# Two room buffers for factors and weights, two steps read ahead, and a late norm vector

## The chip, the cores and the metric

The kernel runs on one core of a Trainium2 chip. The metric is the device time of one launch in microseconds (us), the median over several executions. The engines of the core are called PE (matrix engine, with its weight loads listed apart), VectorE (DVE), ScalarE (ACT), GpSimd (POOL) and SyncE (SP), whose queue issues most of the transfers.

## What is computed

One decoder layer over 1024 prompt tokens and 64 sample tokens, model width 1024. Of the reference these lines matter here:

```
o_diff = diff_attention(...); o_nsa = nsa_attention(...)
mix = jnp.concatenate([o_diff, o_nsa], axis=-1) @ w_out
x = x + rms_norm(mix, g_post_mix)
hm = rms_norm(x, g_pre_mlp)
ff = jnp.square(jax.nn.relu(hm @ w_up)) @ w_down
x = x + rms_norm(ff, g_post_mlp)
```

w_out is 1024 x 1024, w_up 1024 x 4096, w_down 4096 x 1024. All of it is float32.

## The kernel before

Every float32 product is done with operands split in a high and a low part (high by a copy on ScalarE, low by a subtraction on VectorE), and as three matmuls (high-high, high-low, low-high).

The attention fills the time up to about 990 us. Its outputs are written to the DRAM tensor mixT by small stores from tiles named ot. Then three stages follow, and their instructions are interleaved by the framework: it tracks which tile a buffer holds, makes the next user of a buffer wait for the last one of it, and puts each engine's instructions in an order of its own, so that work of the next stage stands among the last of the one before.

1. The out projection, function `phase_out`. There are nine token tiles t = 0..8 (t = 8 has the 64 sample tokens). `weight(k)` loads 128 rows of w_out to a raw tile ur (4 buffers) and splits it in two halves n = 0, 1 of 512 columns: eight k times two n are held as "us" (n = 0, k < 5) or "w" tiles. `front(t)` loads the tile's columns of mixT into a "us" tile of the room pool `rr` and splits it to xm. `prod(t, n)` makes 24 matmuls into the PSUM tile C, and for n = 0 also loads the residual input x into a room tile "us". `post(t)` squares C on ScalarE, normalises, adds x, stores the sum to the DRAM tensor x1d, normalises again to ctmp, and has PE transpose it (T) into xf, the input of the next product.
2. The up product, `phase_up`: a seven-product scheme of fast matrix multiplication over quarters. The x side has factors xc[i, p] for two halves of the tokens p = 0 and 1, seven i each, made by `x_factor` from xf. The w side has a factor W[j, i] per column block j, made from raw w_up tiles and kept in a ring of "us" tiles. Its matmuls write tiles Va to Vd (first block) and Ua to Ud, and its results (squared ReLU) are stored as hF.
3. The down product, `phase_down`, of the same scheme: 96 whole steps of 24 matmuls (Dn) and 32 half ones. A step needs wf (from w_down, tiles eq, qe and q) and hf (from hr, a strip of hF read back; eh is one read early). `load_w` loads blocks of w_down; a dictionary `gate` says at which step each later block may start, by a copy that waits for that step. `load_h(n)` loads hr for step n, and `factor(n)` makes wf and hf.

The x_factor calls for i = 3 and 2 of p = 0 (the last two in the order UORD) stand at the start of phase_up's tail, behind the last post:

```
for i in UORD[5:]:
    self.x_factor(i, 0)
    factor(0, i)
close(0)
```

and their tiles lie in the pool xcb, which opens after `phase_out` has closed its pools.

Of the kernel before, what the change touches and what calls it, by code (L numbers as in the profile page):

```python
# [17 lines left out]
F32 = mybir.dt.float32  # L18
# [45 lines left out]
def f32(ap):  # L64
    return ap.bitcast(F32)
# [60 lines left out]
class Kern:  # L126
# [1108 lines left out]
    def phase_out(self, cl):  # L1235
# [1 line left out]

        nc, A = self.nc, self.A
        w_out = A["w_out"][0]
        ws = []  # L1240
        xins, mhs, pss = {}, {}, {}
        rr = self.rr

        def weight(k):
            raw = rr.tile([P, 4, 256], F32, name="ur", bufs=4).rearrange("p a n -> p (a n)")
            nc.sync.dma_start(raw, w_out[k * P:(k + 1) * P])
            ws.append([])
            for n in range(2):
                c = slice(n * 512, n * 512 + 512)
                if n == 0 and k < 5:  # L1250
                    w = self.wa.tile([P, 2, 4, P], FR, name="us", bufs=5).rearrange("p a k n -> p a (k n)")
                else:
                    w = self.wp.tile([P, 2, 512], FR, name="w")
                self.act_copy(w[:, 0], raw[:, c])
                nc.vector.tensor_sub(w[:, 1], raw[:, c], f32(w[:, 0]))
                ws[-1].append(w)

        def front(t):
            m = self.tok(t)[2]
            mx = rr.tile([P, 2, 4, P], F32, name="us", bufs=3).rearrange("p a b n -> p (a b) n")  # L1260
            nc.sync.dma_start(mx[:, :, :m], self.mixT[:, t * P:t * P + m].rearrange("(k p) t -> p k t", p=P))
            mh = rr.tile([P, 2, 4, QT], FR, name="xm", bufs=2).rearrange("p a b n -> p (a b n)")[:, :2 * KC * P]
            mh = mhs[t] = mh.rearrange("p (a k n) -> p a k n", a=2, k=KC)
            self.act_copy(mh[:, 0, :, :m], mx[:, :, :m])
            nc.vector.tensor_sub(mh[:, 1, :, :m], mx[:, :, :m], f32(mh[:, 0, :, :m]))
            pss[t] = []
# [15 lines left out]
        def prod(t, n):  # L1282
            m = self.tok(t)[2]
            ps = self.psC.tile([P, 512], F32, name="C", tag="C")
            pss[t].append(ps)
            if n == 0:
                xins[t] = rr.tile([P, 2, 4, P], F32, name="us", bufs=3).rearrange("p a b n -> p (a b n)")
                nc.sync.dma_start(xins[t][:m], self.xsrc(t))
            cnt = 0
            for k in range(KC):  # L1290
                for a, b in ((0, 0), (0, 1), (1, 0)):
                    nc.tensor.matmul(ps[:m], mhs[t][:, a, k, :m], ws[k][n][:, b],
                                     start=cnt == 0, stop=cnt == 3 * KC - 1)
                    cnt += 1
# [48 lines left out]
            prod(t, 0)  # L1343
        for t in range(NT - 1, NT + 1):
            prod(t, 1)
            post(t)
            if t < NT:
                self.up_open()
                for i in UORD[:5]:
                    self.up_factor(0, i)  # L1350
# [44 lines left out]
    def up_open(self):  # L1395

        nc, A, rp = self.nc, self.A, self.rr
        w_up = A["w_up"][0]
        raws, S2 = {}, {}
        W = self.W = {}  # L1400

        def load(j):
            raws[j] = []
            for kh in range(2):
                r = rp.tile([P, 4, 256], F32, name="ur", bufs=4)
                nc.sync.dma_start(r, w_up[kh * 512:kh * 512 + 512, j * 256:j * 256 + 256]
                                  .rearrange("(k p) c -> p k c", p=P))
                raws[j].append(r)

        def factor(j, i):  # L1410
            if j == NJ:
                return
            r0, r1 = raws[j]
            q = (r0[:, :, 0:P], r1[:, :, 0:P], r0[:, :, P:256], r1[:, :, P:256])
            n = len(W) % 8
            W[j, i] = w = (self.wa if n < 5 else rp).tile([P, 2, 4, P], FR, name="us", bufs=5 if n < 5 else 3)
            if i == 5:
                S2[j] = rp.tile([P, 4, P], F32, name="s2", bufs=1)
            self.left(q, i, w, nc.vector, nc.vector, S2.get(j, 0))

        self.up_load, self.up_factor = load, factor
        load(0)
        load(1)

    def phase_up(self, close):
# [85 lines left out]
            nxt(2)  # L1511

        for i in UORD[5:]:
            self.x_factor(i, 0)
            factor(0, i)
        close(0)

# [10 lines left out]
    def down_open(self):  # L1528

        nc = self.nc  # L1530
        self.eq = self.early.tile([P, 1, 512], F32, name="eq")
        nc.sync.dma_start(self.eq, self.A["w_down"][0].rearrange("(s e p) c -> e p s c", e=2, p=P)[0, :, 0:1, 0:512])
        self.eh = []
        for sb in range(1):
            h = self.early.tile([P, HT], F32, name=f"eh{sb}")
            nc.sync.dma_start(h, self.hF[DORD[0], sb * P:sb * P + P])
            self.eh.append(h)

    def phase_down(self, qe, qp, fp, psD):
# [19 lines left out]
        def load_w(q, c, gate=None):  # L1559

            r, e = q % 2, q // 2
            s0, s1 = (max(c * 4 - 3, 0), min(c * 4 + 1, NB)) if q == 0 else (c * 4, c * 4 + 4)
            if q == 0 and c == 0:
                t = self.eq
            elif q == 0 and c < 3:
# [8 lines left out]
                (nc.scalar if q == 0 and c < 3 else nc.sync).dma_start(t, w_dn[e, :, s0:s1, r * 512:r * 512 + 512])  # L1574


        def factor(n):
            if n >= len(hr):
                return
            i, sb, p = hr[n]  # L1580
            load_h(n + 4)
            a11, a21, a12, a22 = (quarter.get((q, sb)) for q in range(4))
            v = nc.vector
            if i == 6:
# [39 lines left out]

            return qp.tile([P, 4, 512], F32, name="q03") if n % 3 == 2 else qe.tile([P, 4, 512], F32, name="qe", bufs=2)

        gate = {0: (0, 2), 3: (0, 3), 7: (0, 4)}
        for k, (q, c) in enumerate([(q, c) for q in (1, 3, 2) for c in range(4)]):
            gate[9 + (k % 4) * 4 + (k // 4) * NB] = (q, c)
        R.update(enumerate(self.eh))  # L1630
        load_w(0, 0)
        load_h(1, nc.scalar)
        load_w(0, 1)
        load_h(2, nc.scalar)
        load_h(3, nc.scalar)
        factor(0)
        factor(1)
        for k in range(4):
            acc[k] = qp.tile([P, 4, HT], F32, name=f"acc{k}")
        gp = qp.tile([P, D], F32, name="gpm")  # L1640
# [10 lines left out]
        for n, (i, sb, p) in enumerate(hr):  # L1651
            if n in gate:
                load_w(*gate[n], gate=f32(F[n][0][:, 1, 0:1]))
            if n == 5 * NB:
                nc.sync.dma_start(gp, A["g_post_mlp"].to_broadcast([P, D]))
            factor(n + 2)
            w, h = F.pop(n)
# [228 lines left out]
    def go(self):  # L1886
        with self.pool("base") as base:
# [50 lines left out]
            with ExitStack() as es:  # L1938
# [2 lines left out]

                self.rr = e(self.pool("rr", side="right"))
                self.wa = e(self.pool("wa", side="right"))
                xca = e(self.pool("xca", side="right"))
                self.xstack = [e(ExitStack()) for _ in range(2)]
                self.xc = {}
# [3 lines left out]

                up0 = e(ExitStack())
                self.psU0 = up0.enter_context(self.pool("psU0", side="right", psum=True))
                with self.pool("w2", 11) as self.wp, self.pool("cl") as cl, \
                        self.pool("psC", 3, psum=True) as self.psC, self.pool("psT2", 1, psum=True) as self.psT:
                    self.xtile = xtile
                    self.xca = xca
# [1 line left out]
                early = ExitStack()  # L1958
                self.early = early.enter_context(self.pool("early"))
                with self.pool("xcb") as xcb, ExitStack() as ps:  # L1960
                    for i, p in [(i, 1) for i in UORD[:2]] + [(i, 0) for i in UORD[5:]] + [(i, 1) for i in UORD[2:5]]:
                        xtile(xcb, i, p)
                    for i in UORD[5:]:
                        xtile(self.rr, i, 1, "xm", 2)

# [77 lines left out]
```

## Time and profile before

| | |
|---|---|
| runs before, us | 1824.03 median of 3 (1822.09 to 1831.58) |
| profiled execution, us | 1819.73 |
| its span, us | 1817.9 |
| mean granted clock of PE | 0.969 of full speed |
| PE busy, us (share of the span) | 1709.6 (94%) |
| VectorE busy | 1137.8 (63%) |
| ScalarE busy | 865.4 (48%) |

The profiled execution's time is that of the launch; the span runs from its first to its last instruction. The projection takes from about 972 to 1086 us, the up product from 1075 to 1444, the down product from there to 1803. Of the rows below, a timeline row gives the start in us, the busy time, the engine, the line, the instruction, its tiles (what is written <- what is read) and a count where several run on end; in brackets stands how long the engine was idle ahead of it and who released it.

### The profile page before, as it was taken

The numbers are of one execution on the slowest core, as the hardware profiler recorded it, in microseconds if no ns is written. First come the engines' busy times: TensorE is split into PE (matmuls) and PEld (weight loads), VectorE is DVE, ScalarE is ACT, GpSimd is POOL, SyncE is SP. The second block draws the span as 40 slices with busy tenths as digits, with TensorE's granted clock in tenths as the row PEclk, the third lists the DMA queues.
The fourth block names the chain that finished last, engine by engine and source line by source line (L and its number), as shares of the span: only waits on it lengthen the run. The fifth ranks groups of instructions, "written<-read, shape, count | busy, mean of one in ns | idle before, by whom it ended". The sixth has DMA issues, their size and how long they took to land. (4 is left out here: it accounts for less than half of the span.)

```text
span 1817.9 us, 33390 instructions
## 1 busy us (share of the span) xinstructions
PE 1709.6 (94%) x12155; PEld 1487.3 (82%) x12155; DVE 1137.8 (63%) x2716; ACT 865.4 (48%) x2188; POOL 273.3 (15%) x517
## 2 busy tenths in 40 slices
PE   7689999999998999999989997999999899999997
PEld 7678776677666778787877877999999899999996
DVE  5357667767863575667665478566666456847665
ACT  5244446456762364555555355444444334543442
POOL 1133335334330121212110000000000000000000
PEclk9888899999998999999998998999999999999999
DMA  7531000000203243424245322434443465554334
GB/s 195 115 75 45 14 14 24 7 4 23 58 7 113 86 145 88 120 81 130 65 134 182 129 91 80 140 133 151 145 145 110 159 214 168 177 165 115 106 118 150
DMA packets 193919, 191.92 MB, mean 106 GB/s; under 512 B 32562, under 2 KB 152986, under 8 KB 193754
## 3 DMA queue, kind: packets, MB, share of 16 engines
q1 hardware_dynamic: 191114, 185.10, 33.2%
q10 hardware_dynamic: 2640, 4.68, 0.8%
q8 instruction: 96, 1.57, 0.4%
q14 instruction: 69, 0.57, 0.1%
HBM read 133.75 MB, written 55.97 MB: 104 GB/s over the span
## 5 line engine op out<-in xcount | busy, mean ns | idle before, releaser
L337 PE MATMUL M<-w,xt 128*128 128x384 f32 (+4 forms) x1584 | 293.4, 330 | 15.4 <-ACT natk L139 12.6
L1665 PE MATMUL Dn<-hf,wf 128*128 128x272 f32 x2304 | 292.4, 290 | 10.1 <-ACT hf L139 8.1
L1665 PEld LDWEIGHTS Dn<-hf,wf 128*128 128x128 f32 x2304 | 291.0, 190 | 11.4 <-ACT hf L139 8.4
L337 PEld LDWEIGHTS M<-w,xt 128*128 128x128 f32 (+1 forms) x1584 | 243.8, 191 | 30.2 <-ACT natk L139 13.5
L427 ACT ACTIVATE p<-S,nm 128x512 f32<-128x512 f32 (+3 forms) x288 | 159.9, 561 | 87.8 <-DVE nm L422 48.8
L418 DVE TENSOR_REDUCE nm<-S 128x1 f32<-128x512 f32 (+3 forms) x288 | 148.1, 527 | 59.1 <-PE S L417 39.3
L175 POOL TENSOR_TENSOR rs_r<-rs_t,mhalf 128x1 f32<-128x1 f32 (+2 forms) x64 | 38.2, 599 | 955.1 <-DVE rs_t L173 952.2
L410 PE MATMUL S<-kst,qs 128*128 128x512 f32 (+3 forms) x576 | 162.1, 373 | 9.6 <-ACT p L427 8.6
L481 POOL TENSOR_SCALAR p<-p,coef 128x640 f32<-128x640 f32 (+7 forms) x128 | 92.5, 736 | 150.5 <-DVE coef L478 66.0
L410 PEld LDWEIGHTS S<-kst,qs 128*128 128x128 f32 x576 | 93.8, 194 | 22.6 <-ACT p L427 11.8
L1363 DVE TENSOR_TENSOR us<-ur,us 128x512 fp32r<-128x512 f32 x96 | 66.1, 691 | 66.2 <-ACT us L139 66.1
L139 ACT ACTIVATE us<-ur 128x512 fp32r<-128x512 f32 x101 | 63.4, 629 | 82.3 <-PE Uc L1437 50.4
L1437 PE MATMUL Ub<-xc,us 128*128 128x272 f32 x744 | 101.0, 288 | 0.0
L139 ACT ACTIVATE wf<-q 128x512 fp32r<-128x512 f32 x69 | 43.6, 632 | 116.5 <-PE Dn L1665 108.8
L1437 PE MATMUL Ua<-xc,us 128*128 128x272 f32 x744 | 99.0, 289 | 0.0
L150 DVE COPY pt<-T 128x512 f32<-128x512 f32 (+3 forms) x100 | 61.7, 618 | 55.9 <-PE T L517 42.1
L1437 PEld LDWEIGHTS Ub<-xc,us 128*128 128x128 f32 x744 | 96.1, 188 | 0.0
L1437 PEld LDWEIGHTS Ua<-xc,us 128*128 128x128 f32 x744 | 95.8, 189 | 0.0
L139 ACT ACTIVATE hf<-hr 128x544 fp32r<-128x544 f32 (+1 forms) x127 | 74.9, 590 | 43.8 <-PE Dn L1675 28.1
L139 ACT ACTIVATE pt<-T 128x512 f32<-128x512 f32 (+4 forms) x116 | 60.8, 527 | 69.0 <-PE T L517 41.1
L1363 DVE TENSOR_TENSOR hf<-hr,hf 128x544 fp32r<-128x544 f32 (+1 forms) x127 | 82.0, 648 | 16.0 <-ACT hf L139 15.8
L517 PEld LDWEIGHTS T<-ident,p 128*128 128x128 f32 x528 | 56.5, 141 | 40.7 <-issue 34.6
(363 smaller groups left out, 3351.0 us busy)
## 6 DMA issues: line engine op xcount, KB each, us to landing
hF<-uh SPq DMA_DIRECT2D x105, 272.0 KB
hr<-hF SPq DMA_DIRECT2D x92, 272.0 KB
kvp<-cache_diff_kv SPq DMA_DIRECT2D x128, 128.0 KB
ur<-w_up SPq DMA_DIRECT2D x32, 512.0 KB
q<-w_down SPq DMA_DIRECT2D x13, 1024.0 KB
raw<-w_in SPq DMA_DIRECT2D x32, 192.0 KB
raw<-w_in SPq DMA_DIRECT2D x40, 128.0 KB
hr<-hF SPq DMA_DIRECT2D x32, 136.0 KB
```

Source lines behind the costliest of these rows:

```text
L139: self.nc.scalar.activation(out, in_, AF.Copy, scale=scale)
L150: self.nc.vector.tensor_copy(out, in_)
L175: nc.gpsimd.tensor_tensor(r[:rows], t[:rows], self.mhalf[:rows], op=OP.pow)
L337: nc.tensor.matmul(ps[1][:m, :n], self.xt[c][:, a, k, c0:c0 + m], ws[k][:, b, :n], start=i == 0, stop=i == len(ops) - 1)
L410: nc.tensor.matmul(S[:, a * P - lo:b * P - lo], qs[:, ps, j, :], kst[hf][:, kc, a * P - lo:b * P - lo], start=ps == 0, stop=ps == 1 and no ...
L418: nc.vector.reduce_max(nm[:, n:n + 1], S[:, a * P - lo:b * P - lo], axis=AX.X, negate=True)
L427: nc.scalar.activation(p[:, a * P:b * P], tiles[n][:, a * P - lo:b * P - lo], AF.Exp, bias=nm[:, 0:1], accum_out=sums[:, n:n + 1])
L481: nc.gpsimd.tensor_scalar(v, v, coef[:, sw + 1, j:j + 1], 0.0, op0=OP.mult, op1=OP.add)
L517: nc.tensor.transpose(T[:, m * 256 + jj * P:m * 256 + jj * P + P], st["p", sw, pr * 2 + jj][:, kb * P:(kb + 1) * P], self.ident)
L1363: lo.tensor_sub(w[:, 1], src, f32(w[:, 0]))
L1437: nc.tensor.matmul(ps[:, p, :QT], w[:, a, k, :], x[:, b, k, :], start=start and cnt == 0, stop=cnt == 11, skip_group_check=True)
L1665: nc.tensor.matmul(dps[db][:, q, :QT], w[:, a, db * P:(db + 1) * P], h[:, b, q * QT:(q + 1) * QT], start=st and m == 0, stop=sp and m == 2)
```

## The change

- A new pool `xcA` on the right side holds two tiles "xa" of the size of a factor. First they hold the split weights of w_out for n = 1, k < 4 (two k to a tile), later the factors i = 3, 2 of p = 0. The two x_factor calls are moved ahead of `post(8)`.
- To pay for that, the pool w2 goes from 11 to 7 "w" tiles, and the room pool's "us" ring from 3 to 2 buffers; the ring of W factors from 8 to 7. The five factors of p = 1 take the pool xcb.
- In the down product two strips of w_down (eq with two) and two of hF (eh0 and eh1) are read early, the blocks of w_down for q = 0 are cut one strip later, `gate` is moved to steps 1, 4 and 7, and steps 0 and 1 are made before the load of hr for step 2 is issued.
- The last norm's vector gpm is loaded behind a copy that waits for step 80.

```diff
-                if n == 0 and k < 5:
+                if n == 1 and k < 4:
+                    if k % 2 == 0:
+                        wv = self.xcA.tile([P, 2, 4, QT], FR, name="xa", bufs=2)
+                        wv = wv.rearrange("p a b n -> p (a b n)")[:, :4 * 512]
+                        wvs.append(wv.rearrange("p (x a n) -> p x a n", x=2, a=2))
+                    w = wvs[-1][:, k % 2]
+                elif n == 0 and k < 5:
...
-            mx = rr.tile([P, 2, 4, P], F32, name="us", bufs=3).rearrange("p a b n -> p (a b) n")
+            mx = rr.tile([P, 2, 4, P], F32, name="us", bufs=2).rearrange("p a b n -> p (a b) n")
...
-                xins[t] = rr.tile([P, 2, 4, P], F32, name="us", bufs=3).rearrange("p a b n -> p (a b n)")
+                xins[t] = rr.tile([P, 2, 4, P], F32, name="us", bufs=2).rearrange("p a b n -> p (a b n)")
...
             prod(t, 1)
+            if t == NT:
+                for i in UORD[5:]:
+                    self.xtile(self.xcA, i, 0, "xa", 2)
+                    self.x_factor(i, 0)
             post(t)
...
-            n = len(W) % 8
-            W[j, i] = w = (self.wa if n < 5 else rp).tile([P, 2, 4, P], FR, name="us", bufs=5 if n < 5 else 3)
+            n = len(W) % 7
+            W[j, i] = w = (self.wa if n < 5 else rp).tile([P, 2, 4, P], FR, name="us", bufs=5 if n < 5 else 2)
...
         for i in UORD[5:]:
-            self.x_factor(i, 0)
             factor(0, i)
...
-        self.eq = self.early.tile([P, 1, 512], F32, name="eq")
+        self.eq = self.early.tile([P, 2, 512], F32, name="eq")
...
-        for sb in range(1):
+        for sb in range(2):
...
-            s0, s1 = (max(c * 4 - 3, 0), min(c * 4 + 1, NB)) if q == 0 else (c * 4, c * 4 + 4)
+            s0, s1 = (max(c * 4 - 2, 0), min(c * 4 + 2, NB)) if q == 0 else (c * 4, c * 4 + 4)
...
-        def factor(n):
+        def factor(n, ahead=4):
...
-            load_h(n + 4)
+            if ahead:
+                load_h(n + ahead)
...
-        gate = {0: (0, 2), 3: (0, 3), 7: (0, 4)}
+        gate = {1: (0, 2), 4: (0, 3), 7: (0, 4)}
...
         load_w(0, 0)
-        load_h(1, nc.scalar)
+        factor(0, 0)
+        factor(1, 0)
+        load_h(2, nc.scalar)
         load_w(0, 1)
-        load_h(2, nc.scalar)
-        load_h(3, nc.scalar)
-        factor(0)
-        factor(1)
+        for n in range(3, 6):
+            load_h(n, nc.scalar if n == 3 else nc.sync)
...
             if n == 5 * NB:
+                nc.vector.tensor_copy(gp[:, 0:1], f32(F[n][0][:, 1, 0:1]))
                 nc.sync.dma_start(gp, A["g_post_mlp"].to_broadcast([P, D]))
...
+                self.xcA = e(self.pool("xcA", side="right"))
...
-                with self.pool("w2", 11) as self.wp, self.pool("cl") as cl, \
+                with self.pool("w2", 7) as self.wp, self.pool("cl") as cl, \
...
-                    for i, p in [(i, 1) for i in UORD[:2]] + [(i, 0) for i in UORD[5:]] + [(i, 1) for i in UORD[2:5]]:
-                        xtile(xcb, i, p)
+                    for i in UORD[:5]:
+                        xtile(xcb, i, 1)
```

The new lines move the numbers of what follows by 6 in `phase_out` and 10 in `phase_up`, so that L1292 is L1298 after the change, and L1312 is L1318.

PE's own order at the end of the attention, before. T, o and C are the PSUM tiles of transposes, attention outputs and projection; T and o rows belong to the last attention blocks.

```order
L565 MATMUL T<-ident,jk 128x128
L603 MATMUL T<-ident,p 128x128 x7
L614 MATMUL o<-vst,pt 128x128 x7
L1292 MATMUL C<-us,xm 128x512 x15
L1292 MATMUL C<-w,xm 128x512 x15
L565 MATMUL T<-ident,jk 128x128
L603 MATMUL T<-ident,p 128x128 x4
L1292 MATMUL C<-w,xm 128x512 x18
```

The same place after the change.

```order
L603 MATMUL T<-ident,p 128x128 x4
L1298 MATMUL C<-us,xm 128x512 x12
L603 MATMUL T<-ident,p 128x128 x3
L614 MATMUL o<-vst,pt 128x128 x7
L565 MATMUL T<-ident,jk 128x128
L603 MATMUL T<-ident,p 128x128 x8
L614 MATMUL o<-vst,pt 128x128 x8
L565 MATMUL T<-ident,jk 128x128
L1298 MATMUL C<-xa,xm 128x512
L1298 MATMUL C<-us,xm 128x512 x12
L1298 MATMUL C<-xa,xm 128x512 x11
```

Twelve projection matmuls now stand ahead of the attention's last pieces, and the other 84 of tiles 0 and 1 behind them; before, further C groups of 1, 14, 8 and 25 followed, with the last attention pieces among and behind them.

SyncE's order in the projection, before: the room loads us<-mixT and us<-x_prompt, the stores x1d<-us, with the attention's last stores mixT<-ot.

```order
L1261 DMA us<-mixT 128x8x128
L1406 DMA ur<-w_up 128x4x256
L568 DMA mixT<-ot 128x128
L1406 DMA ur<-w_up 128x4x256 x3
L568 DMA mixT<-ot 128x128
L1288 DMA us<-x_prompt 128x1024
L1309 DMA x1d<-us 128x1024
L1261 DMA us<-mixT 128x8x128
L568 DMA mixT<-ot 128x128
L1288 DMA us<-x_prompt 128x1024
L1309 DMA x1d<-us 128x1024
```

The same place after the change.

```order
L568 DMA mixT<-ot 128x128 x3
L1246 DMA ur<-w_out 128x1024 x4
L1416 DMA ur<-w_up 128x4x256 x4
L1315 DMA x1d<-us 128x1024
L1267 DMA us<-mixT 128x8x128
L1315 DMA x1d<-us 128x1024
L1294 DMA us<-x_prompt 128x1024
L1267 DMA us<-mixT 128x8x128
```

The load of mixT for tile 2 stood ahead of the first store of x1d and now stands behind it, and four loads of w_out stand behind the attention's last store.

PE's order at tiles 7 and 8 after the change; rows with 64x512 are tile 8's, the others tile 7's.

```order
L1298 MATMUL C<-us,xm 128x512 x15
L1298 MATMUL C<-w,xm 128x512 x9
L1323 MATMUL T<-ident,ctmp 128x128 x8
L1298 MATMUL C<-us,xm 64x512 x2
L1298 MATMUL C<-xa,xm 128x512 x12
L1298 MATMUL C<-w,xm 128x512 x6
L1298 MATMUL C<-us,xm 64x512 x13
L1298 MATMUL C<-w,xm 64x512 x9
L1298 MATMUL C<-w,xm 128x512 x6
```

VectorE's order there after the change, from tile 7's xm (128x1024) to tile 8's (128x8x64): L1380 to L1385 and L1373 are x_factor's, L1314 adds the residual, L1318 is the last read of x in post(6).

```order
L1271 TENSOR_TENSOR xm<-us,xm 128x1024
L1380 TENSOR_TENSOR xf_12882<-xf_12882 128x4x272
L1314 TENSOR_TENSOR us<-us,ctmp 128x1024
L1381 TENSOR_TENSOR xf_12882<-xf_12882 128x4x272
L1373 TENSOR_TENSOR xc_12873<-xf_12882,xc_12873 128x1088
L173 TENSOR_SCALAR rs_t<-css 128x1
L1385 TENSOR_TENSOR xf_12882<-xf_12882 128x4x272
L1373 TENSOR_TENSOR xc_12871<-xf_12882,xc_12871 128x1088
L1383 TENSOR_TENSOR xf_12882<-xf_12882 128x4x272
L1318 SCALAR_TENSOR_TENSOR ctmp<-us,rs_r,gpre_12885 128x1024
L1373 TENSOR_TENSOR xc_12874<-xf_12882,xc_12874 128x1088
L1271 TENSOR_TENSOR xm<-us,xm 128x8x64
```

Factor operations stand between tile 7's split and the last read of x that the load of tile 8 waits for.

## Rows read from the trace of the kernel before

**Rows 1.** Page, busy us, share, instructions; PE's waits: us, times, longest.

```profile
PE 1709.6 (94%) x12155; PEld 1487.3 (82%) x12155; DVE 1137.8 (63%) x2716; ACT 865.4 (48%) x2188; POOL 273.3 (15%) x517
...
PE Dn L1665 <- ACT hf L139: 8.1, 1, 8.1
...
PE T L1317 <- DVE ctmp L1312: 5.6, 1, 5.6
PE Vc L1437 <- DVE uh L1486: 5.1, 1, 5.1
```

**Rows 2.** Windows: length, busy us of each engine, PEclk, DMA share, GB/s.

```profile
968.00:972.00 4.00, 3.64 (x18) 3.65 (x18) 3.69 (x10) 3.54 (x10) 0.00 (x0) 0.50 0.82 225
1009.00:1058.00 49.00, 49.00 (x229) 39.92 (x228) 24.30 (x34) 20.63 (x41) 4.38 (x8) 1.00 0.40 129
1086.00:1116.00 30.00, 15.12 (x74) 13.12 (x74) 25.49 (x31) 17.00 (x28) 1.08 (x2) 0.72 0.16 48
1448.00:1456.00 8.00, 0.00 (x0) 0.00 (x0) 3.59 (x6) 2.28 (x4) 0.00 (x0) 0.65 1.04 398
```

**Rows 3.** Timeline of the projection's loop, 1009 to 1023.

```profile
1009.49 1.77 PE L1292 MATMUL C<-us,xm 128*128 128x512 f32 x7
1009.69 0.60 ACT L1302 ACTIVATE ctmp<-C 128x512 f32<-128x512 f32 x1 [4.43 <-PE C L1292]
...
1015.19 0.32 SPq L1309 DMA_DIRECT2D x1d<-us  x1
...
1018.73 0.37 SPq L1261 DMA_DIRECT2D us<-mixT  x1
...
1021.53 1.78 PE L1292 MATMUL C<-us,xm 128*128 128x512 f32 x7
...
1022.83 1.06 ACT L139 ACTIVATE xm<-us 128x1024 fp32r<-128x1024 f32 x1 [0.41 <-DMA us<-mixT]
```

**Rows 4.** Timeline of the attention's end, PE and VectorE.

```profile
965.45 0.97 PE L410 MATMUL S<-kst,qs 128*128 128x512 f32 x2 [2.60 <-ACT p L427]
...
969.05 3.20 PE L614 MATMUL o<-vst,pt 128*128 128x128 f32 x14
971.90 4.01 PE L1292 MATMUL C<-us,xm 128*128 128x512 f32 x15
...
974.30 0.35 DVE L563 SCALAR_TENSOR_TENSOR jk<-od,rs_r,sub 128x128 f32<-128x128 f32 x1 [0.73 <-POOL rs_r L175]
...
991.45 6.08 PE L1292 MATMUL C<-w,xm 128*128 128x512 f32 x25
```

**Rows 5.** Timeline of loads, splits and the attention's last store.

```profile
957.19 3.28 SPq L1246 DMA_DIRECT2D ur<-w_out  x3
...
965.96 2.18 ACT L139 ACTIVATE w<-ur 128x512 fp32r<-128x512 f32 x4
...
999.88 0.32 SPq L568 DMA_DIRECT2D mixT<-ot  x1
```

**Rows 6.** Timeline of the projection's end and the up product's start.

```profile
1071.86 3.98 PE L1292 MATMUL C<-w,xm 128*128 128x512 f32 x16
...
1080.06 5.80 PE L1292 MATMUL C<-w,xm 128*64 128x512 f32 x24
...
1099.17 6.09 DVE L1363 TENSOR_TENSOR xc<-xf,xc 128x1088 fp32r<-128x1088 f32 x5
...
1112.49 3.09 PE L1437 MATMUL Vc<-xc,us 128*128 128x272 f32 x12 [5.06 <-DVE uh L1486]
```

**Rows 7.** Timeline where the down product starts.

```profile
1444.94 3.02 PE L1665 MATMUL Dn<-hf,wf 128*128 128x272 f32 x22 [0.24 <-DVE hf L1363]
...
1449.02 0.35 ACTq L1557 DMA_DIRECT2D hr<-hF  x1
...
1455.39 0.66 ACT L139 ACTIVATE hf<-hr 128x544 fp32r<-128x544 f32 x1 [4.71 <-DMA hr<-hF]
...
1456.10 10.08 PE L1665 MATMUL Dn<-hf,wf 128*128 128x272 f32 x62 [8.13 <-ACT hf L139]
```

More of the change, by code (lines that the diff above doesn't have):

```diff
@@ L1239, in phase_out @@
         w_out = A["w_out"][0]
-        ws = []
+        ws, wvs = [], []
         xins, mhs, pss = {}, {}, {}
@@ L1530, in down_open @@
         nc = self.nc
-        self.eq = self.early.tile([P, 1, 512], F32, name="eq")
-        nc.sync.dma_start(self.eq, self.A["w_down"][0].rearrange("(s e p) c -> e p s c", e=2, p=P)[0, :, 0:1, 0:512])
+        self.eq = self.early.tile([P, 2, 512], F32, name="eq")
+        nc.sync.dma_start(self.eq, self.A["w_down"][0].rearrange("(s e p) c -> e p s c", e=2, p=P)[0, :, 0:2, 0:512])
         self.eh = []
-        for sb in range(1):
+        for sb in range(2):
             h = self.early.tile([P, HT], F32, name=f"eh{sb}")
```

## Prediction

> **What bounds it now.** The page and the list of PE's waits first [rows 1]: the matrix engine (PE) is busy 94% of the span, so a change is worth what it does to PE's gaps, and the list names those around it: 8.1 us for the first factor of the second product's second step (hf), 5.6 us for the last token tile's norm (ctmp), 5.1 us for a vector operation (uh). What surrounds them must be read too, since the change takes buffers from it. While projection tiles are computed PE has no gap at all: 49.00 of 49 us busy at clock 1.00 [rows 2], one tile every 12.04 us (1009.49 to 1021.53, [rows 3]). The tiles before are mixed into the attention's tail: PE does 15 projection matmuls from 971.90 on and goes on with them among the attention's last pieces [rows 4], whose last output is only stored at 999.88 [rows 5]. So the stages overlap, and there is little to spare.
>
> **The end of the attention.** The weights of the output's second half, k=0..3, now go to the new tiles "xa". These lie where the attention's last tiles (od, jk, ot) lie, so their first writer on ScalarE waits for the landing of the attention's last store. What is late next: the four raw buffers "ur" stay full until these splits are done, and the loads of w_out for k=4..7, three of which were issued at 957.19 [rows 5], stand behind them. Their splits ended before at 968.14 (965.96 + 2.18, [rows 5]); now PE has only 12 projection matmuls to do before the attention is over, as the order shows, against all 96 of two tiles before (15+15+18+1+14+8+25 in the order shown). Without those in front the tail shrinks. It is two passes of transposes, o matmuls, norm, transpose: the pass before ran from the o group that ends at 972.25 to its normed jk at 974.65 [rows 4]: 2.4 us, with T, ScalarE copies and o about 5 us a pass. Two passes from 972 on, I estimate the last store at 982 and landed at 984.2 (a store of 512 KB is done within 3.5 us, [rows 3]; this one is a small block), the first xa split at 984.8, the first load behind the splits issued at 985.6 and landed at 989.7 (4.1 us, as the mixT loads below). PE takes up the projection at 984.8 with 84 of the 96 matmuls left, at 5.80/24 = 0.2416 us each [rows 6]: 20.3 us, and the weights of k=4 are there when it comes to them. It loses about 2 us more to the clock, which was granted at 0.50 in 968 to 972 [rows 2] after PE had stood for 2.60 us at 965.45 [rows 4]. So tiles 0 and 1 are finished at 1007.1, against 997.5 before (991.45 + 6.08, [rows 4]): **+9.6**. If all of the tail's length could be hidden it is 0; if the tail stays as long as it was (999.88), +25.
>
> **The loop over tiles.** The "us" ring in the room falls from 3 to 2. The tile's residual input x takes the buffer that its mixT tile just left, so with two the load of mixT(t+2) must wait until post(t) has stored its x1d and read its last x. With three it was the load for t+3, a whole tile earlier than needed. From [rows 3], post(t) begins at 1009.69 (0.2 behind the end of tile t), x1d is issued at 1015.19, L1312 reads x for the last time, the mixT load is issued at 1018.73: 9.0 us. In between lay one low-part operation (L1265) of some 1.2 us (an xc's is 6.09/5 = 1.22 at nearly the same size, [rows 6]), which by the new order comes later, so 7.8. From issue to ScalarE's xm 4.1 (1018.73 to 1022.83), 1.06 for xm, 1.2 for its low part: with the 0.2, 14.4 us from the end of tile t to the third matmul of t+2, the first to need the low part. Tile t+1 has covered 12.04 of them and two matmuls 0.5. So every second tile chain is 14.4 + 11.8 = 26.2 us for two tiles, 13.1 each: **+1.05 a tile**. At the start it is worse: tiles 0 and 1 end within one half-tile of each other (mixed k by k), so t=2 waits for post(0). The last 32 matmuls of the 96 are t=1's, so tile 0 ends at 1007.1 - 32 x 0.2416 = 999.4, and the third matmul of t=2 comes at 999.4 + 14.4 = 1013.8: PE is idle for about 5 us, then slow (2 us). With 46 matmuls (11.1) and the transposes, tile 2 ends at 1027.2 against 1009.6 [rows 3]: +17.6. Four more tiles at +1.05, rounded down to 3.8, make **+21.4** at the end of t=6: 1079.2 against 1009.6 + 4 x 12.04 = 1057.8. The mixT price has a rule beside the row: the Trainium skill, DMA: Bandwidth & Descriptors (the two cost components) gives about 2.0 us fixed plus bytes over 436 GB/s, so 3.2 us for these 512 KB against 4.1 here; with it the loop would lose 0.6 a tile and t=2 start 0.9 earlier, some 3 us less in all. The sum keeps the row.
>
> **Tiles 7 and 8.** Before, their loads were an entire tile ahead too. Now the load for t=7 waits for post(5)'s last read and that for t=8 for post(6)'s, and in both posts VectorE and ScalarE do factors of the first product in between, in the order shown. Tile 5 ends at 1066.5 (1027.2 + 3 x 13.1); 14.4 on, and some 3.6 for three such operations (1.22 each, the xc group, [rows 6]), tile 7 starts in earnest at 1084.5, PE idle for 2.6 and then slow. post(6) begins at 1079.4; its last read would end some 7.6 on (the 9.0 of [rows 3], less the 1.2 and 0.2 to the issue), but xm's low part and five or six operations of factors come first, 7.5 us: 1094.6. The load for t=8 has half the size; at 3.5 us it lands at 1098.3. On PE two matmuls of t=8 stand ahead of 18 of t=7's second half, and 22 more ahead of its last 6. So t=7 waits for t=8's load: split 0.6, 48 matmuls at 0.2416 (11.6), 2 of slow clock, end at 1112.5 against 1075.84 (1071.86 + 3.98, [rows 6]), **+36.9** in all, of which some 8 is slow clock. The least for this step is +1 a tile as in the loop, 13 less; nothing in it can be a gain.
>
> **First product.** Gains begin here. x factors 3 and 2 need only tokens known by t=7, and are now made before post(8), on ScalarE and VectorE while PE computes t=8. Before, they were in the row of five xc (6.09 us, [rows 6]) behind the last transposes, and PE stood in the 5.1-us wait of [rows 6] at 1112.49, with other gaps there, 14.9 of 30 us between 1086 and 1116 [rows 2]. Two factors cost VectorE 2 x 1.22 and two subtractions of 1.28, 5.0 us. The p=1 factors after t=8 still need their own 17 us of VectorE, under 40 matmuls more. I take **-5.65** (0 if VectorE is late with them anyway; -8.5 if more than half of the gaps go).
>
> **Second product.** Step 0 runs 1444.94 to 1447.96 and PE waits until 1456.10 [rows 7] for hf: its load is issued at 1449.02 behind ScalarE's copies, and lands at 1455.39 beside two megabyte loads (DMA share 1.04 in 1448 to 1456, [rows 2]). Now two steps are read ahead, PE gets 3.02 us more work, but the load for step 2 stands behind a ScalarE copy that waits for the end of step 1 (24 matmuls on). Issued near 1451, 3.5 to 6.4 us to land, step 2 begins near 1455.5 where step 1 began at 1456.10: 3.02 + 0.6 = **-3.6** (-2 to -7). The last norm's vector, the 2-strip eq, fewer w2 buffers (11 to 7, four of whose weights are in xa) and the 7-ring of left factors I cost at nothing: the gpm load now starts at step 80 and is first read behind step 98, so 18 steps of 3.02 us hide the 4 us of a load, and w2 has no more to hold. Were that cover gone, gpm would cost its 4 us. If the ring of 7 were short, one left factor's copy of some 0.55 (2.18/4, [rows 5]) would stand open now and then.
>
> **The sum.** +36.9 up to the end of tile 7, which holds all terms before it, -5.65, -3.6 and 0 for the rest make **+27.7**. The profiled execution took 1819.73 us (span 1817.9); its sum is 1847.4. The runs shown lie at 1822.09 to 1831.58, median 1824.03, 2.4 to 4.3 above, so a median of 1850. 0.5% is 9.1 us, about what a measurement of this kernel tells from no change.
>
> **Rivals.**
> (a) *The intended one, faster.* Loads hidden: the t+2 load lands in under 11.5 us after post(t) begins (ScalarE and VectorE run it early, 1.2 us or more below my 14.4, and the tail needs no w loads). Then losses are only the start's 2 to 3 us at most, and -5.65 -3.6 or, at the upper ends, -8.5 -7 stay: 1808 to 1817. For it: 4.1 us holds some idle queue time. Against it: [rows 3] gives 14.4 with no idle of VectorE in it. It decides where the post-to-xm path is below 12.5 us. 0.10.
> (b) *Nothing to be measured.* Start and loop cost about 10, and both gains give it back: 1816 to 1832. It needs tiles 7 and 8 not to stall. 0.13.
> (c) *Half of it.* Start and loop as computed, but tiles 7 and 8 lose no clock: +10 to +20, 1833 to 1843. 0.22.
> (d) *My forecast*, +20 to +36, 1843 to 1860. 0.47.
> (e) *Worse.* Each gap of 1 to 2 us in the loop lets the clock fall, as the 2.6-us one did: 6 tiles x 1.5 more, 1860 to 1872. 0.07.
> The range 1827 to 1862 leaves out (a), part of (b) and (e), under 2 in 10. Slower by over 0.5% are (c) to (e) and the tail of (b): 0.77; within 0.5% 0.12; faster 0.11.
>
> **What would show it.** In the new profile: 12 projection matmuls and then none until the last mixT store; PE's waits naming xm or mixT before C in every tile, 1 to 2 us each, and a long one (10 us) before t=8; clock below 1 in 1009 to 1110; the Vc wait of 5.1 and half of the hf wait of 8.1 gone. If C runs back to back in the loop, the loss is not there and I am wrong.

## The result and the profile after

| | before | after |
|---|---|---|
| median, us | 1824.58 (1822.09 to 1831.58, 4 runs) | 1848.83 (1842.31 to 1854.47, 4 runs) |
| ratio after to before | | 1.0130, 95% interval 1.0107 to 1.0154 |
| profiled execution, us | 1819.73 | 1845.14 |

The changed kernel is slower, by 24 us in this comparison and by 27 in a later one (1848.46 against 1821.36, ratio 1.0144, 1.0117 to 1.0172); both intervals lie above 1. The page of the kernel after:

```profile
span 1843.4 us, 33368 instructions
...
PE 1722.8 (93%) x12155; PEld 1493.9 (81%) x12155; DVE 1140.1 (62%) x2717; ACT 867.3 (47%) x2188; POOL 276.2 (15%) x517
```

PE is busy 13.2 us longer than before (1722.8 against 1709.6, [rows 1]) for the same number of instructions, and the span is 25.5 us longer (1843.4 - 1817.9): about half of the loss is matmuls that took longer, the other half is idle PE. The mean granted clock was 0.965 against 0.969. The list of PE's waits after (total, times, longest, us):

```profile
PE C L1298 <- ACT xm L139: 7.8, 6, 2.5
PE T L1323 <- DVE ctmp L1318: 7.6, 2, 3.9
...
PE Dn L1676 <- ACT hf L139: 6.4, 1, 6.4
...
PE T L565 <- DVE jk L563: 4.9, 3, 2.3
...
PE C L1298 <- ACT xa L139: 2.7, 1, 2.7
```

The first line and the fifth are new: projection matmuls wait six times for xm, the split of a mixT load, and once for xa. The fourth line, the attention's last transposes waiting for jk, was 0.4 us before. The 8.1 of the second product's wait in [rows 1] has become 6.4, and the 5.1-us wait of Vc is gone. For ctmp there was one wait of 5.6 at tile 8's norm; now there are two, 3.9 ahead of tile 8's matmuls and 3.6 at its norm.

**One event to count from.** The profiled executions differ before the changed code begins, so times are counted here from one event at the attention's end: the last transpose of a 64x64 block of jk, called J. It stands at 950.47 in the trace of before:

```profile
950.47 0.24 PE L565 MATMUL T<-ident,jk 64*128 64x64 f32 x1
```

and at 948.08 in that of after (first row below). The table gives the us from J to the end of the last matmul of a token tile, to the first Dn, and to the first of the second product's half steps (the first run of 28 Dn<-hf,q), each worked out from start and time of the row in the timeline, as 999.47 + 2.96 - 948.08 = 54.4 for tile 1.

| us from J | tile 1 | tile 2 | tile 6 | tile 7 | tile 8 | first Dn | half steps |
|---|---|---|---|---|---|---|---|
| before | 47.1 | 59.2 | 107.3 | 125.4 | 135.4 | 493.8 | 796.2 |
| after | 54.4 | 72.6 | 125.0 | 157.6 | 167.6 | 521.9 | 824.0 |
| after less before | +7.3 | +13.4 | +17.7 | +32.2 | +32.2 | +28.1 | +27.8 |
| after, profiled again | 54.1 | 72.2 | 124.1 | 157.0 | 167.0 | 521.3 | 825.2 |
| two rooms on before | 48.8 | 60.4 | 113.8 | 145.3 | 155.4 | 514.2 | 813.9 |
| three rooms, xa, early factors | 52.0 | 64.0 | 111.9 | 129.9 | 139.9 | 493.6 | 796.1 |
| late weights in xa | 60.8 | 76.9 | 129.1 | 161.1 | 171.2 | 524.8 | 825.6 |

Read along the third row: 7.3 are lost by the end of tile 1, 6.1 at tile 2, 4.3 over tiles 3 to 6, 14.5 at tile 7; 4.1 come back in the first product and 0.3 in the second. The second profile of the same kernel differs from the first by up to 1.0 us until the first Dn and by 1.3 at the half steps, so a term under 1 us can't be told from this spread. From the half steps to the end it is 71.3 us in all three profiles, so the late load of the last norm's vector costs nothing.

**The attention's end**, timeline of PE, ScalarE and SyncE after:

```profile
948.08 0.24 PE L565 MATMUL T<-ident,jk 64*128 64x64 f32 x1
...
961.94 3.02 PE L1298 MATMUL C<-us,xm 128*128 128x512 f32 x12
...
976.46 0.30 PE L565 MATMUL T<-ident,jk 128*128 128x128 f32 x1 [2.25 <-DVE jk L563]
...
977.10 0.32 SPq L568 DMA_DIRECT2D mixT<-ot  x1
978.79 2.19 ACT L139 ACTIVATE xa<-ur 128x512 fp32r<-128x512 f32 x4 [1.71 <-DMA mixT<-ot]
...
979.47 0.79 PE L1298 MATMUL C<-xa,xm 128*128 128x512 f32 x1 [2.71 <-ACT xa L139]
...
980.17 2.13 SPq L1246 DMA_DIRECT2D ur<-w_out  x4
...
999.47 2.96 PE L1298 MATMUL C<-w,xm 128*128 128x512 f32 x12
```

The attention's last store is issued at 977.10, xa is split at 978.79, PE's first projection matmul on xa starts 2.71 us late, and only then the last four loads of w_out go out (980.17), three of which had been issued at 957.19 before [rows 5]. Up to J + 31 PE has done 12 matmuls of the projection here. With so little to mix in, it also stands 4.9 us in all for jk (0.4 before), ahead of the attention's last transposes.

**The loop**, timeline of tiles 4 and 5 after:

```profile
1038.65 0.32 SPq L1315 DMA_DIRECT2D x1d<-us  x1
...
1042.07 0.37 SPq L1267 DMA_DIRECT2D us<-mixT  x1
...
1046.25 1.06 ACT L139 ACTIVATE xm<-us 128x1024 fp32r<-128x1024 f32 x1 [4.95 <-DMA us<-mixT]
1047.21 0.58 ACT L1308 ACTIVATE ctmp<-C 128x512 f32<-128x512 f32 x1
...
1047.36 0.73 PE L1298 MATMUL C<-us,xm 128*128 128x512 f32 x2 [0.81 <-ACT xm L139]
...
1055.68 0.37 SPq L1267 DMA_DIRECT2D us<-mixT  x1
```

From one mixT load to the next it is 1055.68 - 1042.07 = 13.6 us, where [rows 3] had a tile each 12.04 us. Note the order on ScalarE: xm (for the tile ahead, 1046.25) stands before the second square of the tile just finished (L1308, 1047.21). So load, xm, square, the post's chain and the next load follow each other in one ring: 4.18 from issue to xm, 0.96 to the square, 8.47 from the square to the next issue. PE is just the engine that waits: its first two matmuls start at 1047.36. No run here turns that order round, so what the order alone costs is not shown.

**Tiles 7 and 8** after:

```profile
1080.13 0.32 SPq L1315 DMA_DIRECT2D x1d<-us  x1
...
1082.71 3.87 POOL L175 TENSOR_TENSOR rs_r<-rs_t,mhalf 128x1 f32<-128x1 f32 x1 [7.85 <-DVE rs_t L173]
...
1086.61 1.28 DVE L1318 SCALAR_TENSOR_TENSOR ctmp<-us,rs_r,gpre 128x1024 f32<-128x1024 f32 x1 [0.44 <-POOL rs_r L175]
...
1087.97 0.37 SPq L1267 DMA_DIRECT2D us<-mixT  x1
1088.04 1.08 PE L1323 MATMUL T<-ident,ctmp 128*128 128x128 f32 x4 [3.94 <-DVE ctmp L1318]
...
1091.46 0.62 ACT L139 ACTIVATE xm<-us 128x512 fp32r<-128x512 f32 x1
...
1092.14 1.12 PE L1298 MATMUL C<-us,xm 128*64 128x512 f32 x2 [1.20 <-ACT xm L139]
...
1101.99 3.65 PE L1298 MATMUL C<-w,xm 128*64 128x512 f32 x15
...
1112.73 2.96 PE L1298 MATMUL C<-w,xm 128*64 128x512 f32 x12
```

The residual is stored at 1080.13, but x is read for the last time only at 1086.61 (6.5 us later; in the loop 2.07 lie between the store at 1038.65 and L1318 at 1040.72), behind the factor operations of the order shown above. So the load for tile 8 goes out at 1087.97, and with it 18 matmuls of tile 7 wait. PE's longest wait there, 3.94 us, is for the same L1318: post(6)'s transposes of ctmp stand ahead of those matmuls. In the same stretch GpSimd's small rs_r took 3.87 us, where the eight others between 1050 and 1140 took 0.54 or 0.55; of that, L1318 waited only the 0.44, since three factor operations stood ahead of it on VectorE in that time. Windows of the same stretches (length, busy us of PE, PEld, DVE, ACT, POOL; granted clock, DMA share, GB/s):

```profile
1030.00:1058.00 28.00, 25.38 (x116) 19.83 (x115) 11.05 (x16) 9.12 (x18) 2.20 (x4) 1.00 0.37 121
1058.00:1090.00 32.00, 24.00 (x101) 17.85 (x100) 21.68 (x25) 15.08 (x28) 5.52 (x4) 0.89 0.29 96
1073.07:1105.64 32.57, 24.30 (x90) 16.89 (x89) 19.26 (x24) 13.08 (x24) 4.42 (x2) 0.79 0.20 63
```

PE stands 2.6 of 28 us in the loop at clock 1.00, then 8 of 32 us at 0.89; before it stood 0 of 49 at 1.00 [rows 2]. The third window runs from tile 6's end to tile 7's, where the kernel before took 18.02 us, all busy, at clock 1.00: of the 14.5 us lost there, 8.3 (32.57 - 24.30) are idle PE and 6.3 (24.30 - 18.02) slower matmuls, at a granted clock of 0.79.

**The second product's start** after:

```profile
1469.96 6.17 PE L1676 MATMUL Dn<-hf,wf 128*128 128x272 f32 x48
...
1476.18 0.90 ACTq L1566 DMA_DIRECT2D hr<-hF  x2
...
1481.81 0.66 ACT L139 ACTIVATE hf<-hr 128x544 fp32r<-128x544 f32 x1 [5.01 <-DMA hr<-hF]
...
1482.52 9.72 PE L1676 MATMUL Dn<-hf,wf 128*128 128x272 f32 x63 [6.38 <-ACT hf L139]
```

48 matmuls (two steps) run on end where 24 did [rows 7], and the wait for hf of step 2 is 6.38 us. Its load is issued at 1476.18, after the second step, and takes 5.6 us.

### The profile page after: what moved, and what is told of

Read it like the earlier page. It is cut to its first block, busy times and chain, and to the rows that moved or that the text cites. A ratio compares the mean times of both kernels' runs of the same rounds, so it can differ in the third digit from the quotient of the medians.

```text
span 1843.4 us, 33368 instructions
## 1 busy us (share of the span) xinstructions
PE 1722.8 (93%) x12155; PEld 1493.9 (81%) x12155; DVE 1140.1 (62%) x2717; ACT 867.3 (47%) x2188; POOL 276.2 (15%) x517
## 5 line engine op out<-in xcount | busy, mean ns | idle before, releaser
L337 PEld LDWEIGHTS M<-w,xt 128*128 128x128 f32 (+1 forms) x1584 | 244.9, 191 | 28.1 <-ACT natk L139 11.5
L1373 DVE TENSOR_TENSOR us<-ur,us 128x512 fp32r<-128x512 f32 x96 | 66.1, 690 | 70.7 <-ACT us L139 70.7
L1373 DVE TENSOR_TENSOR hf<-hr,hf 128x544 fp32r<-128x544 f32 (+1 forms) x126 | 81.2, 646 | 20.0 <-ACT hf L139 19.9
```

The costliest lines, as they stand in the source:

```text
L337: nc.tensor.matmul(ps[1][:m, :n], self.xt[c][:, a, k, c0:c0 + m], ws[k][:, b, :n], start=i == 0, stop=i == len(ops) - 1)
L1373: lo.tensor_sub(w[:, 1], src, f32(w[:, 0]))
```

## The experiments

**Rooms alone.** On the kernel before:

```diff
-... name="us", bufs=3)   (mixT and x_prompt)
+... name="us", bufs=2)
-            n = len(W) % 8
+            n = len(W) % 7
```

> The kernel before with only the room ring cut from 3 to 2 and the ring of W factors from 8 to 7; no xa tiles, no moved factors, nothing in the down product. Theory A (the two rooms are the larger part of the loss, by the waits for mixT at tiles 2 to 8): 10 to 20 us slower than before, ratio 1.006 to 1.011, with PE waits on xm in the projection loop of 5 us or more in sum. Rival B (the late weights in xa, which lie on the attention's tiles, make the loss, the rooms little): at most 3 us slower, ratio up to 1.002.

Measured: 1844.46 against 1820.28 us, ratio 1.0128 (1.0102 to 1.0153). More than theory A's 10 to 20: the rooms alone give nearly the whole change of the medians. PE waits 4.4 us in all for xm's split on ScalarE, and 0.5 for that on VectorE. PE's timeline:

```profile
956.08 0.25 PE L565 MATMUL T<-ident,jk 64*128 64x64 f32 x1
...
1043.03 0.60 PE L1317 MATMUL T<-ident,ctmp 128*128 128x128 f32 x4
1044.14 0.74 PE L1292 MATMUL C<-us,xm 128*128 128x512 f32 x2 [0.51 <-ACT xm L139]
...
1056.39 0.60 PE L1317 MATMUL T<-ident,ctmp 128*128 128x128 f32 x4
...
1084.73 0.63 PE L1317 MATMUL T<-ident,ctmp 128*128 128x128 f32 x4 [3.29 <-DVE ctmp L1312]
...
1088.26 1.11 PE L1292 MATMUL C<-us,xm 128*64 128x512 f32 x2 [1.09 <-ACT xm L139]
```

A tile takes 1056.39 - 1043.03 = 13.4 us, with the wait for xm ahead of each, and before tile 8 PE waits 3.29 us for ctmp and then for xm. From the table: +1.7 at tile 1, +6.5 at tile 6, +19.9 at tile 7, +20.4 at the first Dn, of the changed kernel's +28.1. That is less than the medians say; J came at 956.08 in this execution, 5.6 us later than in the one of before, and whether the change has a part in that, one profile of before can't tell. Rival B is out either way.

**Three rooms, the rest kept.** The changed kernel with `bufs=3` and the ring of 8, and down_open and phase_down as before, which makes the space:

> The changed kernel with 3 rooms and the ring of 8 again, and the down product as before (which makes the space for the third room); the xa weights and the early factors stay. Theory A: only the start's loss of 5 to 8 us and the first product's gain of some 4 us stay, so -2 to +6 us against before, ratio 0.999 to 1.003, and no PE waits on xm in the loop. Rival B (late weights): the loss stays at 15 us or more, ratio 1.008 or more.

Measured: 1821.54 against 1820.28 us, ratio 1.0003 (0.9984 to 1.0021); and measured again:

> The three-room kernel with xa and early factors and the down product as before, again: ratio to before 0.998 to 1.002, with the start 5 us later and the first product some 4.6 us shorter than before, counted from the last 64x64 transpose of jk.

1823.72 against 1823.82, ratio 0.9988 (0.9971 to 1.0005). PE's timeline of the first:

```profile
961.47 0.24 PE L565 MATMUL T<-ident,jk 64*128 64x64 f32 x1
...
991.25 0.80 PE L1298 MATMUL C<-xa,xm 128*128 128x512 f32 x1 [0.89 <-ACT xa L139]
...
1010.55 2.96 PE L1298 MATMUL C<-w,xm 128*128 128x512 f32 x12
...
1098.39 2.94 PE L1298 MATMUL C<-w,xm 128*64 128x512 f32 x12
```

C runs on end from tile 2 on, there is no wait for xm in its list of waits, and the loss is +5.0 at tile 1 and no more (+4.5 at tile 8). At the start PE stands 4.9 us for jk, as in the changed kernel, and only 0.9 for xa, so most of this price goes with the few matmuls that are mixed into the attention's end. Then the first product gives 4.6 back: -0.2 at the first Dn. In the repeat it was 494.54 - 140.46 = 354.1 us from tile 8 to the first Dn, against 358.4 before: 4.3. So xa and the moved factors together cost 5 us at the start and earn 4 to 5 after it.

**The down product as before**, else the changed kernel, measured twice, the second time beside the changed kernel:

> The changed kernel with the down product as before (one strip read early, old gates, gpm early). Theory A (steps read ahead gain little at the end, 0.3 us in the two traces, most of it given back at the first change of factor): the same as the changed kernel within 3 us, ratio to before 1.012 to 1.016. Rival C (the read-ahead is worth its 3.6 us and more): 4 to 7 us slower than the changed kernel, ratio 1.016 or more.

> The changed kernel with the down product as before, again. Theory A (reading two steps ahead gains nothing that lasts): within 2 us of the changed kernel. Rival C (it is worth its 3.6 us): 3 to 5 us slower than it.

> The changed kernel again, beside the one with the down product as before, on one chip. Ratio to before 1.011 to 1.015 by either theory.

Measured: 1848.72 (ratio to before 1.0150, 1.0121 to 1.0179), and beside the changed kernel 1850.19 against 1848.46 (1.0155 and 1.0144 to the same runs of before, with intervals that overlap and are wider than the 3.6 us looked for). In the second pair's two profiles, the first Dn to the half steps took 1776.26 - 1472.28 = 303.98 us with two steps read ahead and 1776.73 - 1472.73 = 304.00 with one. The lead is there at first: the 769 matmuls up to the first change of factor end in a wait for wf, whose end comes 1579.55 - 1472.28 = 107.3 us after the first Dn with two steps ahead

```profile
1579.55 1.15 PE L1676 MATMUL Dn<-hf,wf 128*128 128x272 f32 x7 [2.38 <-DVE wf L1373]
...
1578.00:1590.00 12.00, 9.76 (x53) 9.54 (x54) 8.49 (x15) 3.66 (x8) 0.00 (x0) 0.72 0.54 181
```

and 1582.76 - 1472.73 = 110.0 us with one:

```profile
1582.76 1.15 PE L1674 MATMUL Dn<-hf,wf 128*128 128x272 f32 x7 [2.45 <-DVE wf L1373]
...
1578.00:1590.00 12.00, 8.86 (x69) 8.43 (x68) 11.05 (x19) 6.16 (x12) 0.00 (x0) 1.00 0.34 114
```

So 2.8 us ahead, and both lose the same 2.4 us there. Behind it the granted clock was 0.72 in the first and 1.00 in the second, 53 matmul records in 12 us against 69, and the lead was gone. In the first profiles of the changed kernel and the one before, the changed kernel alone waited for wf at that place,

```profile
1576.47 1.14 PE L1676 MATMUL Dn<-hf,wf 128*128 128x272 f32 x7 [1.32 <-DVE wf L1373]
```

and the granted clock behind it was 0.86 (1577 to 1589) against 1.00 (1553 to 1565 before). But the ring-of-7 kernel below, without the read-ahead, also waited there (1.80 us) and had 0.86 in 1558 to 1570, and the late-weights kernel, with it, waited 0.27 and had 1.00 in 1585 to 1597. Over all profiles of the study that stretch took 302.1, 300.8 and 304.0 us with the read-ahead, and 298.6 to 304.9 in the eleven without: the spread is larger than the gain looked for, and the means are 302.3 and 302.0. Rival C is not borne out, though the medians alone don't exclude it; that the wait for wf and the clock eat the lead is seen in two pairs, and not shown to be the rule.

**Late weights in xa.** The changed kernel with one condition turned:

```diff
-                if n == 1 and k < 4:
+                if n == 1 and k >= 4:
```

> The changed kernel with the last weights (n = 1, k = 4 to 7) in the xa tiles in place of the first four, so that no load of w_out and no split of the first half stands behind the attention's last store. Theory A: the start's share of the loss goes, 5 to 8 us faster than the changed kernel, ratio to before 1.008 to 1.011, while the room waits at tiles 2 to 8 stay. Rival B: the loss goes nearly whole, ratio 1.003 or less. Rival D (attention's end is bound by its own chain, the weights don't matter): as the changed kernel, ratio 1.012 or more.

Measured: 1855.98, ratio 1.0196 (1.0165 to 1.0226), 7 us slower in its median than the changed kernel, by ratios whose intervals hardly overlap, and 2.9 us slower from J at the first Dn. A and B are out; D has the ratio right (1.012 or more), but it said as the changed kernel. PE's timeline:

```profile
997.10 0.30 PE L565 MATMUL T<-ident,jk 128*128 128x128 f32 x1 [2.25 <-DVE jk L563]
1001.35 5.29 PE L1298 MATMUL C<-xa,xm 128*128 128x512 f32 x12 [3.94 <-ACT xa L139]
...
1013.74 2.94 PE L1298 MATMUL C<-xa,xm 128*128 128x512 f32 x12
```

The framework now mixes 60 projection matmuls into the attention's end, as the kernel before does, so the attention's last transpose comes at J + 41.2 (997.10 - 955.92) in place of J + 28.4, and the last 36 matmuls of tiles 0 and 1 wait for that store: tile 1 ends at J + 60.8. So here the weights that wait for the attention's last store gained nothing by being needed late, since the work mixed into the attention's end made that store later.

**Where the 13 us at tile 7 come from.** Two tries on the two-room kernel. First, the five factors' calls moved behind post(7):

> The kernel before with two rooms and the ring of 7, as in the first run of this study, and the five first x factors, which stand behind post(5) and post(6), moved behind post(7). From one attention event (the last 64x64 transpose of jk) to the end of tile 7 the two-room kernel took 19.9 us longer than the kernel before, 13.4 of them behind tile 6. Theory A (VectorE's factor work between the posts delays the last reads that the loads for tiles 7 and 8 wait for): those 13.4 fall to 5 or less, and the first product starts later by what the factors take, so that the whole is no faster than the two-room kernel. Rival E (the loads' own chain does it, with PE's order): they stay at 10 or more.

Measured: 1843.31, ratio 1.0126. The framework put every engine's instructions in the same order as without the move, row for row, so this was the two-room kernel once more and the question stayed open. In this pair counting from J repeats within 0.2 us: tiles 6, 7 and 8 at 113.7, 145.2 and 155.3, as in the first. Second, the factors left out:

```diff
-                    self.x_factor(i, 0)
+                    nc.gpsimd.memset(f32(self.xc[i, 0]), 0.0)
```

> The two-room kernel (rooms and ring cut on the kernel before) with the five first x factors left out: their tiles are filled by a memset on GpSimd, so VectorE and ScalarE do nothing for them behind post(5) and post(6), and the first product's values are not the reference's. In the two-room kernel 13.4 us are lost between the ends of tiles 6 and 7. Theory A (the factor work in between delays the last reads that the loads for tiles 7 and 8 wait for): at most 5 us are lost there. Rival E (the chain from post to load to split alone does it, with PE's order of tile 8 ahead of tile 7's second half): 10 us or more.

One profile, 1843.72 us. Here the stretch from tile 6 to tile 7 took 146.1 - 119.6 = 26.5 us, against 31.5 with the factors and 18.0 in the kernel before, so 8.4 are lost in place of 13.5. Neither expectation is met. With the order that the framework gave this kernel, 5 us went with the factor work and 8.4 stayed with the chain, since

```profile
1080.95 1.28 DVE L1312 SCALAR_TENSOR_TENSOR ctmp<-us,rs_r,gpre 128x1024 f32<-128x1024 f32 x1 [0.73 <-POOL rs_r L175]
...
1082.79 0.37 SPq L1261 DMA_DIRECT2D us<-mixT  x1
...
1086.60 1.11 PE L1292 MATMUL C<-us,xm 128*64 128x512 f32 x2 [3.04 <-ACT xm L139]
```

the load for tile 8 still goes out only after post(6)'s last read, and PE waits 3.04 us for its xm ahead of tile 7's second half. (At tile 3 this kernel stalls by itself, which the framework's new order made; the whole time says nothing of the factors.)

**The ring of W factors alone** at 7, on the kernel before:

> The kernel before with the ring of W factors at 7 in place of 8 and three rooms as before. Theory A (the ring is hidden): within 3 us of before, ratio 0.998 to 1.002. Rival F (the ring is a part of the two-room kernel's loss): 4 us or more slower, ratio 1.002 or more.

Measured: 1825.52 against 1821.36, ratio 1.0019 (1.0002 to 1.0037). The medians, 4.2 us apart, lie on the edge of both expectations. From J the first Dn came at 1448.36 - 953.83 = 494.5, 0.7 later than before; the rest lies in the second product's spread. In this run the room's part of the ring still has three buffers. But the two-room kernel, which has both cuts, takes 514.2 - 155.4 = 358.8 us from tile 8 to the first Dn, where the ring is in use, and the kernel before 358.4. So the ring is at most a small part of the two-room kernel's loss.

**Another order of pools**, on the three-room kernel:

> The three-room kernel with xa and early factors (down product as before), with the pools on the right side opened in the order wa, rr, xcA, xca in place of rr, wa, xcA, xca, so that other tiles come to lie on the attention's last ones; the order of PE at the attention's end stays nearly the same. Theory A (what costs the start 5 us is that PE has only 12 projection matmuls to mix into the attention's end): as the three-room kernel, ratio to before 0.998 to 1.002. Rival G (the address of xa alone matters): the start's 5 us go, 4 us or more faster than before, ratio 0.998 or less.

> The three-room kernel with the other pool order, again, beside the three-room kernel on one chip. If its gain of 0.4% holds: ratio to before 0.994 to 0.998 and some 4 us faster than the three-room kernel. If it was chance (its start was no faster, its up product 2.4 us and its down product 3.7 us faster than the three-room kernel's, where their instructions are nearly the same): ratio 0.998 to 1.002, as the three-room kernel.

Measured: first 1817.36 against 1825.02, ratio 0.9962 (0.9939 to 0.9985), then 1821.27 against 1823.82, ratio 0.9985 (0.9964 to 1.0005). The first ratio is the one that rival G named, but the gain didn't hold to a size that can be told from none, and the start was no earlier either time: tile 1 at J + 51.7 and J + 53.5 ((1000.66 + 2.96) - 951.97 and (1005.66 + 2.96) - 955.12). No kernel of the study beats the one before for certain.

## Why the prediction was right, step by step

The forecast was 1850 us, the median 1848.83. The mechanism held in the main up to the second product, with the loop's picture wrong in part. That the sum comes out within 0.1 us is luck: the terms are off by up to 3.3 us and cancel, and the second profile gives 29.1. Forecast and measured from J, with the changed kernel's second profile in the last column (both less the one profile of before):

| step | forecast | measured | again |
|---|---|---|---|
| attention's end, tile 1 | +9.6 | +7.3 | +7.0 |
| tile 2 | +8.0 | +6.1 | +6.0 |
| tiles 3 to 6 | +3.8 | +4.3 | +3.7 |
| tiles 7 and 8 | +15.5 | +14.5 | +14.9 |
| first product | -5.65 | -4.1 | -4.1 |
| second product | -3.6 | -0.3 | +1.6 |
| sum | +27.7 | +27.8 | +29.1 |

- **Attention's end.** I put the last store at 982, 31.5 us behind J; it came at 977.10, 29.0 behind J. The tail and its 12 matmuls were as said. The price was less, since the store came 2.5 us earlier and landed within 1.7 us. The 4.9 us for jk lie in the tail's length that I reckoned with.
- **Tile 2.** As computed, post(0) came late and tile 2 with it. The runs show something I had not said: this 6.1 belongs to neither part alone. With two rooms alone tile 2 follows tile 1 after 11.6 us, with xa alone after 12.0, with both after 18.2: xa lets tiles 0 and 1 end close together, and two rooms make tile 2 wait for tile 0's post. At the first Dn the two parts alone come to 20.4 - 0.2 = 20.2, both together to 28.1; most of the difference arises at tile 2.
- **The loop.** The size was right and the picture wrong. I had two chains side by side, of 26.2 us for two tiles. The trace shows one ring through ScalarE, 13.6 us per tile, because xm stands ahead of the second square there. The load's price held (4.18 us from issue to xm, 4.1 forecast). Tile 3 had no wait (11.5 us), tiles 4 to 6 took 13.9, 13.6 and 13.4, so the sum came out near.
- **Tiles 7 and 8.** Right within 1 us: the last read at 1086.61, the load at 1087.97, tile 7's second half behind tile 8's first matmuls. Two slips in the working: 1112.5 - 1075.84 is 36.7, not 36.9, and 1084.5 - 1079.2 less two matmuls (0.5) and eight transposes (1.2) leaves 3.6 us of idle ahead of tile 7, not 2.6; 2.4 were measured (0.89 + 1.51). The one long wait ahead of tile 8 (10 us) that I named as a sign came as three, 3.94, 0.69 and 1.20.
- **First product.** Gain 4.1 twice, and 4.6 and 4.3 in the three-room kernel, where 5.65 was forecast; Vc's wait for uh is gone, but new ones for xc of p = 1 (2.7 and 2.1 us in the list) have come in its place.
- **Second product.** This step failed. The two steps read ahead do run on end, and ahead of the first change of factor the changed kernel led by 2.8 us in one pair of profiles. But I took a lead at the start for a gain at the end, and behind that change it was gone: -0.3 and +1.6 in place of -3.6. The wait for hf fell to 6.4, not to half of 8.1. Why the lead doesn't last stays open; in both of its profiles a wait for wf and a lower clock stand there.

Of the rivals, (b) would have needed tiles 7 and 8 not to stall, and (c) no slow clock there; the clock was 0.89 in 1058 to 1090. In (e) the gaps of 1 to 2 us in the loop were to lower the clock; they didn't: it was granted at 1.00 in 1030 to 1058, where I had named a clock below 1 in all of 1009 to 1110 as a sign. And rival (a), with the rooms' loss taken away and without the read-ahead, is the three-room kernel: gains and start come out even there, not faster.

## What to carry to other kernels

Before a buffer of a ring is given away, write down the ring's whole chain, with each engine's order in it (load, split, square, norm, store, next load), and compare its length with the time that one tile takes on the engine that must not wait: here the longer ring (13.6 against 12.04 a tile, 4.3 us) and the stall it brings at tile 7 (14.5 us) cost more than the 4 us that the space bought. A tile that lies on the last stage's tiles can be written first when that stage's last store has landed, so check what else is queued behind its first write, and what work is left to mix into that stage's end. When a kernel's executions differ before the changed code, count from an event just ahead of it, and profile twice to see how well that repeats.

## What was not expected of the hardware

- The profiled executions reached J at 948.1 to 961.5 us, 13 us apart, though before and after have the same instructions in the same order on every engine up to there; 23 runs of the kernel before, taken together, lay at 1813.62 to 1832.51 us. From J on, the two-room kernel's two profiles agree within 0.2 us up to tile 8, the changed kernel's within 1.0 us, and the two with the other order of pools differ by 1.9 us at tile 1.
- Around a gap of 2.4 us in the second product the granted clock was 0.72 (1578 to 1590) in one execution, and 1.00 in the same window of another with a gap as long at the same place.
- A GpSimd operation on one value per partition (rs_r) took 3.87 us at tile 7, and 0.55 us elsewhere in the loop, by the profile's record; VectorE worked without a gap through the first 3.5 us of it. It took 3.87 at the same place in the two-room kernel, and 0.55 throughout where the factors were left out.
